# Layer 0's norm products on GpSimd, negated sines on ScalarE, six table stores for eight

## The chip, the cores and the metric

The kernel runs on one core of a Trainium2 chip. The metric is the device time of one execution in microseconds; the time shown is the median of several runs. The core's engines are TensorE (PE, matrix products), VectorE (DVE), ScalarE (ACT), GpSimd (POOL) and SyncE (SP), which issues nearly all transfers here. Each engine works through its own queue in order.

## The reference

A two-layer encoder on 2048 tokens of width 1024. Each layer takes `hn = rms_norm(x, norm_gain)`, projects it to 4096 columns, runs a banded attention over eight heads of 64 and a chunked retention with rotary phases over four heads of 128, gates both, and adds the product with `w_out` to `x`. A last norm ends it. The two pieces that the change touches are these:

```python
def rms_norm(x, gain=None):
    xf = x.astype(jnp.float32)
    y = xf * lax.rsqrt(jnp.mean(xf * xf, axis=-1, keepdims=True) + EPS)
    if gain is not None:
        y = y * gain.astype(jnp.float32)

def rotary_tables(positions, dim):
    inv_freq = 1.0 / (ROPE_BASE ** jnp.linspace(0.0, 1.0, dim // 2, dtype=jnp.float32))
    ang = positions.astype(jnp.float32)[:, None] * inv_freq[None, :]
    return jnp.cos(ang), jnp.sin(ang)
```

## The kernel before

The 2048 tokens are 16 tiles of 128 (tokens 0 to 15 in the names: `rsn_9` belongs to tile 9). Four tiles make a column block of 512, so a layer has four blocks, n = 0 to 3. Weights come in sections; for each section and block PE computes `dT` (L731, columns of the projection as rows, for queries and keys) and then `dV` (L752, values and gates). The attention and retention of the block before run in between, in thirds. Every f32 operand of a matrix product is split into a high and a low half in f16, `hi` on ScalarE and `lo` = value minus hi on VectorE.

The normed tokens of layer 0 are made once, in section 0, ahead of the block that uses them. For one tile of 128 x 1024: ScalarE squares and sums a row (`sq`), VectorE scales the sum (L210) and GpSimd raises it to the power -1/2 (L212), which gives the root factor `rsn`; then VectorE multiplies x by the row's factor and by the gain `gb` (`mul`, L254 or L1207), in place; ScalarE writes hi (L227 or L269), VectorE lo (L231 or L276), and SP transposes both by DMA into the block's tiles `hTh` and `hTl` (L236, L237). Tiles 0 to 3 take a way of their own through PE, which the change leaves. Tiles 4 to 7 are steps `x...4` to `x...7` in a string of step names that is the order of the program's start (L1388 on), and tiles 8 to 15 come from `norms_from_input` (L1192), where a list gives each tile's steps one round each, interleaved with attention and retention.

Rotary needs a cosine and a signed sine table per block, 128 x 512 each. `tables` (L84) computes angles of 256 positions on each of two halves of 64 partitions, reduces them in steps on VectorE (L93 to L119), takes sine and cosine on ScalarE (L121, L122), negates the sine on VectorE (L124), and stores to device memory by eight stores of 64 x 256 (L129 to L132): the cosine twice, the negated and the plain sine once each, for both halves. `dense_T` loads them back as `tabc` and `tabs` (L616, L617); the rotary products with them are L670, with `swp`, the swapped halves. There are four such sets, for n = 0 to 3.

PE, ACT, DVE and POOL execute in the order of the code. SP's order is the code's as far as the end of the first block's `dV`, and after that a planner places the transfers by its own costs.

What else the prediction names: `S` scores (L800), their maximum `mq` (L804, L806), the exponents (L807) and halves `pq` on ScalarE (L809) and GpSimd (L810), transposes `pT` of them by SP (L812); gates `v`, `rv`, `gt` (ACT L760 to L763, DVE L766 to L770), which free the accumulator that the next `dV` needs; `sh`, the retention state's halves (L864, L868), and `rss` its root (L920, L921).

Of the kernel before, what the change touches and what calls it, by code (L numbers as in the profile page):

```python
# [12 lines left out]
AF = mybir.ActivationFunctionType  # L13
ALU = mybir.AluOpType
# [13 lines left out]
def hybrid_trunk(ctx: ExitStack, tc: tile.TileContext, x, pos, gain, gcol, w_in, w_out, rel, fgain,  # L28
# [8 lines left out]
    act, dve, pool, pe, sp = nc.scalar, nc.vector, nc.gpsimd, nc.tensor, nc.sync  # L37
# [32 lines left out]
    tab_d = [dp.tile([2, P, 512], F32, tag=f"tab{n}", name=f"tab{n}") for n in range(NS)]  # L70
# [12 lines left out]
    def tables(n, wk):  # L83

        ang, k, r, k2 = wk
        pi = k2.bitcast(I32)
        for hf in range(2):
            o = n * 512 + hf * 256
            sp.dma_start(pi[hf * 64:(hf + 1) * 64, :], pos[None, o:o + 256].to_broadcast([64, 256]))
        yield  # L90

        def mulsub(dst, kk, c):
            dve.scalar_tensor_tensor(out=dst, in0=kk, scalar=-c, in1=dst, op0=ALU.mult, op1=ALU.add)  # L93

        def rnd(dst, src, mul):
            dve.tensor_scalar(dst, src, mul, MAGIC, op0=ALU.mult, op1=ALU.add)
            dve.tensor_scalar(dst, dst, -MAGIC, None, op0=ALU.add)

        dve.tensor_copy(ang, pi)
        dve.tensor_scalar(ang, ang, invf_sb[:, 0:1], None, op0=ALU.mult)  # L100
        yield
        rnd(k, ang, 1.0 / P1)
        yield
        for c in (PA, PB, PC):
            mulsub(ang, k, c)
            yield
        dve.tensor_scalar(k2, k, -(PD + PE_), None, op0=ALU.mult)
        dve.tensor_tensor(k2, k2, ang, op=ALU.add)
        yield
        rnd(k2, k2, 1.0 / TWO_PI)  # L110
        yield
        for kk, c in ((k2, QA), (k, PD), (k2, QB), (k, PE_), (k2, QC)):
            mulsub(ang, kk, c)
            yield
        dve.tensor_scalar(ang, ang, PI_CL, -PI_CL, op0=ALU.min, op1=ALU.max)
        dve.tensor_scalar(k, ang, HALF_PI, -TWO_PI, op0=ALU.is_gt, op1=ALU.mult)
        yield
        dve.tensor_tensor(k, k, ang, op=ALU.add)
        dve.tensor_scalar(k, k, HALF_PI, PI_CL, op0=ALU.add, op1=ALU.min)  # L119
        yield  # L120
        act.activation(r, ang, AF.Sin)  # L121
        act.activation(k2, k, AF.Sin)  # L122
        yield
        dve.tensor_scalar(ang, r, -1.0, None, op0=ALU.mult)  # L124
        yield
        for hf in range(2):
            sl = slice(hf * 64, hf * 64 + 64)
            cs = slice(hf * 256, hf * 256 + 256)
            sp.dma_start(tab_d[n][0, 0:64, cs], k2[sl, :])  # L129
            sp.dma_start(tab_d[n][0, 64:128, cs], k2[sl, :])  # L130
            sp.dma_start(tab_d[n][1, 0:64, cs], ang[sl, :])
            sp.dma_start(tab_d[n][1, 64:128, cs], r[sl, :])  # L132
        tab_done.add(n)
        yield

# [18 lines left out]
    gains = {}  # L154
# [48 lines left out]
    def squares(xt, nm, junk):  # L203
        ss = b2.tile([P, 1], F32, tag="ss", name=f"ss{nm}", bufs=4)
        act.activation(junk, xt, AF.Square, accum_out=ss)
        return ss

    def rms_of(ss, m, e, nm):

        dve.tensor_scalar(ss, ss, m, e, op0=ALU.mult, op1=ALU.add)  # L210
        rs = b2.tile([P, 1], F32, tag="rs", name=f"rs{nm}", bufs=4)
        pool.tensor_tensor(rs, ss, mhalf, op=ALU.pow)  # L212
        return rs

    def hT_of(l, n):
        if (l, n) not in hT:
            hT[l, n] = (hp.tile([P, KT, 512], F16, tag="hTh", name=f"hTh{l}_{n}"),
                        hp.tile([P, KT, 512], F16, tag="hTl", name=f"hTl{l}_{n}"))
        return hT[l, n]

    def row_pair(nm):
        return (b2.tile([P, 1280], F16, tag="sc", name=f"rh{nm}")[:, 0:D],
                b2.tile([P, 1280], F16, tag="pq", name=f"rl{nm}")[:, 0:D])

    def rows_hi(rows, xt, s_=None):

        act.activation(rows[0], xt, AF.Copy, scale=1.0 if s_ is None else s_[:, 0:1])  # L227

    def rows_lo(rows, xt, s_=None):
        if s_ is None:  # L230
            dve.tensor_tensor(rows[1], xt, rows[0], op=ALU.subtract)  # L231
        else:
            dve.scalar_tensor_tensor(out=rows[1], in0=xt, scalar=s_[:, 0:1], in1=rows[0], op0=ALU.mult, op1=ALU.subtract)

    def transpose_rows(rows, dh, dl):
        sp.dma_start_transpose(out=dh, in_=rows[0])  # L236
        sp.dma_start_transpose(out=dl, in_=rows[1])  # L237

    class Tok:
# [11 lines left out]
            self.r = rms_of(self.ss, gains[0].m, gains[0].e, self.nm)  # L251

        def mul(self):
            dve.scalar_tensor_tensor(out=self.x, in0=self.x, scalar=self.r[:, 0:1], in1=gains[0].b, op0=ALU.mult,  # L254
                                     op1=ALU.mult)

# [9 lines left out]
        def hi(self):  # L266
            if self.rows:
                self.rw = (self.rows[:, 0:D], self.rows[:, D:2 * D])
                act.activation(self.rw[0], self.x, AF.Copy)  # L269
                return  # L270
            for h in range(2):
                act.activation(self.hh[:, h * KT // 2:(h + 1) * KT // 2, :], self.pt[h], AF.Copy)

        def lo(self):
            if self.rows:
                dve.tensor_tensor(self.rw[1], self.x, self.rw[0], op=ALU.subtract)  # L276
                return
            for h in range(2):
                ks = slice(h * KT // 2, (h + 1) * KT // 2)
                dve.tensor_tensor(self.hl[:, ks, :], self.pt[h], self.hh[:, ks, :], op=ALU.subtract)  # L280
# [871 lines left out]
    def push(gen, steps):  # L1152
        bg.append([gen, steps])
# [36 lines left out]
    def norms_from_input(ts, spaces, tab):  # L1190

        def load(k):  # L1192
            u = us[k]
            u.x = spaces[k] if spaces else w4.tile([P, D], F32, tag="w4", name=f"xin{u.t}")
            sp.dma_start(u.x, x[u.t * P:(u.t + 1) * P, :])

        def sq(k):
            u = us[k]
            u.h = [h_[:, :, u.t % 4 * P:(u.t % 4 + 1) * P] for h_ in hT_of(0, u.t // 4)]
            u.ss = squares(u.x.rearrange("p (k c) -> p k c", c=P), u.nm, u.h[0])  # L1200

        def root(k):
            us[k].rs = rms_of(us[k].ss, gains[0].m, gains[0].e, us[k].nm)

        def mul(k):
            u = us[k]
            dve.scalar_tensor_tensor(out=u.x, in0=u.x, scalar=u.rs[:, 0:1], in1=gains[0].b, op0=ALU.mult, op1=ALU.mult)  # L1207

        def hi(k):
            us[k].rows = row_pair(us[k].nm)  # L1210
            rows_hi(us[k].rows, us[k].x)

        def lo(k):
            rows_lo(us[k].rows, us[k].x)

        def dma(k):
            transpose_rows(us[k].rows, *us[k].h)

        us = []
        for t in ts:  # L1220
            u = St()
            u.t, u.nm = t, f"n0_{t}"
            us.append(u)
        plan = {0: [lambda: load(0)]}
        add = lambda r, fn, k: plan.setdefault(r, []).append(lambda: fn(k))
        for k in range(4):
            if k:
                add(4 * k - 4, load, k)
            for i, fn in enumerate((sq, root, mul, hi, lo, dma)):
                add(3 + 4 * k + i, fn, k)  # L1230
        for r in range(21):
            for fn in plan.get(r, ()):
                fn()
            next(tab, None)
            yield
        for _ in tab:
            yield
# [58 lines left out]
    gain_load(0)  # L1296
    sp.dma_start(invf_sb, invf)
    t0 = tables(0, [gp.tile([P, 256], F32, tag="gt", name=f"wk{i}") for i in range(4)])
    go_on(t0)
    W.load(0)  # L1300
# [77 lines left out]
    def do(names):  # L1378
        for nm in names.split():
            steps[nm]()  # L1380

    def rounds(lists):
        for names in lists:
            do(names)
            yield
# [1 line left out]
    do("xsq0 xrs0 t xmul0 t t t t xtr0 Wsq0 xhi0 Wlp0 Wsc0 xsq1 xlo0 Whi0 xrs1 xsq2 Wlo0 t xsq3 xmul1 d Wsq1 xrs2 xrs3 xtr1 "  # L1387
# [3 lines left out]
    g00.vdone = 4  # L1391
    push(rounds(["xhi4 xrs5 xrs6", "xlo4 xmul5 xrs7", "xdma4 xhi5 xmul6 bt", "xlo5 xhi6 u", "xdma5 xlo6 xmul7", "xdma6 xhi7",
                 "xlo7", "xdma7 u", "u u bt", "u u bt", "u u", "u u bt"]), 12)
    att = [None]
    for l in range(DEPTH):
        gO = [Grp(), Grp()]
        go = Grp()
        for s in range(NSW):
            g = grp(l, s)
            for n in range(NS):  # L1400
# [6 lines left out]
                if n == 0 and not first:  # L1407
                    bs, bt = bias_scratch(l, s), bias_tiles(l, s, g)
# [21 lines left out]
                if n == NS - 1 and s == NSW - 1:  # L1430
                    us = []
# [108 lines left out]
```

## Time and profile before

| what | value |
|---|---|
| runs | 2083.72, 2083.68, 2080.86 us, median 2083.68 |
| profiled execution | 2085.9 us, its span 2084.1 |
| PE busy | 2005.3 us, 96% |
| VectorE busy | 1345.9 us, 65% |
| ScalarE busy | 1141.0 us, 55% |
| GpSimd busy | 435.8 us, 21% |
| stretch that the change touches | from 0 to about 215 us |

Times are microseconds from the start of the span. In a row of the timeline, the first number is the start, the second the length, then engine, line, operation, destination and sources, and shape; in brackets stands how long the engine was idle before and what ended that. SPq rows are issues of transfers, whose length is the issue and not the transfer. In a row of waits the numbers are the total, the count and the longest.

### The profile page before, as it was taken

The page shows a single profiled execution, that of the slowest core. Times are in us where ns is not written, and L with a number is a line of the kernel's source. Part 1 is how long each engine was busy: PE and PEld are TensorE (multiplying, and loading weights), DVE is VectorE, ACT ScalarE, POOL GpSimd, SP SyncE. Part 2 cuts the span into 40 slices and gives each one's busy share as a digit, 9 for nine tenths or more (in the row PEclk, how much of TensorE's full clock was granted, in tenths as well). Part 3 has the DMA queues.
Part 4 walks back from the last instruction along what each step waited for, and adds up shares of the span by engine and source line. Part 5 has one row for each costly group of instructions (what it writes and reads, how often), then busy time and mean ns, then how long its engine had stood idle before and what let it go on. Part 6 is the DMA issues. An engine that isn't in the chain of part 4 may idle for free. (4 is left out here: it accounts for less than half of the span.)

```text
span 2084.1 us, 39559 instructions
## 1 busy us (share of the span) xinstructions
PE 2005.3 (96%) x14014; PEld 1051.2 (50%) x14014; DVE 1345.9 (65%) x4031; ACT 1141.0 (55%) x2522; POOL 435.8 (21%) x509
## 2 busy tenths in 40 slices
PE   6888999999999999999999999999999999999998
PEld 4334454555555555544444555555555555555443
DVE  7677666666666666676654667666666666667643
ACT  7455565556565654565444546554655665446432
POOL 1022221222122222231000222222222222222100
PEclk9999999999999999999999999999999999999999
DMA  8767775557567764699875556655755766557874
GB/s 250 169 121 164 142 158 113 120 102 158 121 147 147 158 158 99 134 221 256 219 187 118 121 102 138 134 120 102 149 125 125 174 153 166 121 117 176 212 199 124
DMA packets 645702, 313.65 MB, mean 150 GB/s; under 512 B 459232, under 2 KB 602080, under 8 KB 645504
## 3 DMA queue, kind: packets, MB, share of 16 engines
q1 hardware_dynamic: 645504, 311.12, 66.3%
q8 instruction: 110, 1.80, 0.4%
q14 instruction: 88, 0.72, 0.1%
HBM read 123.26 MB, written 41.98 MB: 79 GB/s over the span
## 5 line engine op out<-in xcount | busy, mean ns | idle before, releaser
L810 POOL TENSOR_TENSOR pq<-sc,pq 128x640 f16<-128x640 f32 (+4 forms) x256 | 324.7, 1269 | 1165.6 <-issue 625.4
L807 ACT ACTIVATE sc<-sc,mq,cT 128x640 f32<-128x640 f32 (+4 forms) x256 | 218.5, 853 | 552.0 <-DVE mq L806 416.9
L731 PE MATMUL dT<-hTh,whT 128*128 128x512 f16 x1008 | 351.5, 385 | 15.8 <-DMA hTh<-hTl 9.7
L752 PE MATMUL dV<-whV,hTh 128*128 128x512 f16 x1024 | 352.9, 380 | 10.0 <-DVE gt L770 9.9
L752 PE MATMUL dV<-whV,hTl 128*128 128x512 f16 x1024 | 353.0, 380 | 0.0
L752 PE MATMUL dV<-wlV,hTh 128*128 128x512 f16 x1024 | 352.7, 380 | 0.0
L731 PE MATMUL dT<-hTh,wlT 128*128 128x512 f16 x1008 | 346.6, 379 | 0.0
L731 PE MATMUL dT<-hTl,whT 128*128 128x512 f16 x1008 | 346.6, 379 | 0.0
L752 PEld LDWEIGHTS <-hTh 128*128 128x128 f16 x2048 | 196.6, 98 | 223.1 <-DVE gt L770 13.7
L731 PEld LDWEIGHTS <-whT 128*128 128x128 f16 x2016 | 193.2, 98 | 223.8 <-issue 26.9
L804 DVE CUSTOM_DVE_ANT_0 sc<-S,bias 128x640 f32<-128x640 f32 (+4 forms) x256 | 188.6, 737 | 70.5 <-PE S L801 64.5
L809 ACT ACTIVATE pq<-sc 128x640 f16<-128x640 f32 (+4 forms) x256 | 171.5, 670 | 10.5 <-DMA pT<-pq 2.5
L1129 PE MATMUL dO<-whO,yly 128*128 128x512 f16 x448 | 170.3, 380 | 2.2 <-DMA yly<-rly 1.5
L1129 PE MATMUL dO<-whO,yhy 128*128 128x512 f16 x448 | 170.3, 380 | 0.4 <-DMA yhy<-hTh 0.4
L1129 PE MATMUL dO<-wlO,yhy 128*128 128x512 f16 x448 | 170.2, 380 | 0.0
L752 PEld LDWEIGHTS <-hTl 128*128 128x128 f16 x1024 | 99.5, 98 | 104.0 <-issue 1.4
L731 PEld LDWEIGHTS <-wlT 128*128 128x128 f16 x1008 | 97.3, 98 | 101.8 <-issue 1.1
L800 PE MATMUL S<-k,q 128*128 128x128 f16 (+3 forms) x592 | 143.3, 268 | 1.9 <-DVE mq L804 1.8
L1129 PEld LDWEIGHTS <-yhy 128*128 128x128 f16 x896 | 87.5, 98 | 101.9 <-issue 1.1
L820 PE MATMUL o<-v,pT 128*128 128x65 f16 x1120 | 130.4, 194 | 8.1 <-DMA pT<-pq 7.6
L821 PE MATMUL o<-v,pT 128*128 128x64 f16 x1120 | 130.6, 195 | 0.0
L801 PE MATMUL S<-k,q 128*128 128x128 f16 (+3 forms) x592 | 130.4, 268 | 0.0
(361 smaller groups left out, 3412.0 us busy)
## 6 DMA issues: line engine op xcount, KB each, us to landing
q<-qq SPq DMA_DIRECT2D x128, 128.0 KB, 2.6
yyy<-y_d SPq DMA_DIRECT2D x32, 512.0 KB, 4.7
stT<-in_w_in_dram SPq DMA_DIRECT2D x27, 512.0 KB, 4.6
stV<-in_w_in_dram SPq DMA_DIRECT2D x26, 512.0 KB, 4.6
k<-kk SPq DMA_DIRECT2D x128, 64.0 KB, 2.0
swp<-rot SPq DMA_DIRECT2D x64, 128.0 KB, 2.5
tabc<-tab SPq DMA_DIRECT2D x32, 256.0 KB, 2.7
tabs<-tab SPq DMA_DIRECT2D x32, 256.0 KB, 2.9
```

Source lines behind the costliest of these rows:

```text
L731: pe.matmul(ps, w_[:, j, kt, :], h_[:, kt, :], start=(m == 0), stop=(m == 23))
L752: pe.matmul(ps, h_[:, kt, a * P:(a + 1) * P], w_[:, kt, :], start=(m == 0), stop=(m == 23))
L800: pe.matmul(o, st.q[:, hx, 0, cs], k_, start=True, stop=False)
L801: pe.matmul(o, st.q[:, hx, 1, cs], k_, start=False, stop=True)
L804: dve.tensor_tensor_reduce(out=v, in0=S[:, 0:w], in1=g.bias[hx][:, 640 - w:640], scale=1.0, scalar=-3.0e38, op0=ALU.add, op1=ALU.max, accu ...
L807: act.activation(v, v, AF.Exp, bias=m[:, 0:1], scale=g.c[:, 0:1])
L809: act.activation(pq[:, 0:w], v, AF.Copy)
L810: pool.tensor_tensor(pq[:, w:2 * w], v, pq[:, 0:w], op=ALU.subtract)
L820: pe.matmul(o[:, 0:65], u.p[:, b, :], v_[:, 0:65], start=(b == 0), stop=False)
L821: pe.matmul(o[:, 0:64], u.p[:, b, :], v_[:, 65:129], start=False, stop=False)
L1129: pe.matmul(ps, h_[:, kt, :], w_[:, kt, :], start=(m == 0), stop=(m == 23))
```

## The change

For tiles 4 to 15 the product with the gain moves from VectorE to GpSimd, and it no longer contains the row's factor: GpSimd computes x times gain in place, right behind the square (ahead of the root instead of behind it). The row's factor enters as a scale of the split: hi is ScalarE's copy with scale r, and lo is VectorE's (x times r) minus hi in one instruction. For each of the four table sets the sine's negation is a ScalarE copy with scale -1 behind the two sines, in place of a VectorE instruction two steps later. The cosine's two stores become one of 64 x 2 x 256 with the source doubled, so a set has six stores instead of eight.

```diff
         act.activation(r, ang, AF.Sin)
         act.activation(k2, k, AF.Sin)
-        yield
-        dve.tensor_scalar(ang, r, -1.0, None, op0=ALU.mult)
-        yield
+        act.activation(ang, r, AF.Copy, scale=-1.0)
+        yield
+        yield
+        d = tab_d[n].rearrange("i (b p) (a c) -> i b a p c", b=2, a=2)
         for hf in range(2):
             sl = slice(hf * 64, hf * 64 + 64)
-            cs = slice(hf * 256, hf * 256 + 256)
-            sp.dma_start(tab_d[n][0, 0:64, cs], k2[sl, :])
-            sp.dma_start(tab_d[n][0, 64:128, cs], k2[sl, :])
-            sp.dma_start(tab_d[n][1, 0:64, cs], ang[sl, :])
-            sp.dma_start(tab_d[n][1, 64:128, cs], r[sl, :])
+            sp.dma_start(d[0, :, hf].rearrange("b p c -> p b c"), k2[sl, None, :].to_broadcast([64, 2, 256]))
+            for b, t_ in enumerate((ang, r)):
+                sp.dma_start(d[1, b, hf], t_[sl, :])
...
         def mul(self):
+            if self.rows:
+                pool.tensor_tensor(self.x, self.x, gains[0].b, op=ALU.mult)
+                return
...
-                act.activation(self.rw[0], self.x, AF.Copy)
+                rows_hi(self.rw, self.x, self.r)
...
-                dve.tensor_tensor(self.rw[1], self.x, self.rw[0], op=ALU.subtract)
+                rows_lo(self.rw, self.x, self.r)
...
         def mul(k):
-            u = us[k]
-            dve.scalar_tensor_tensor(out=u.x, in0=u.x, scalar=u.rs[:, 0:1], in1=gains[0].b, op0=ALU.mult, op1=ALU.mult)
+            pool.tensor_tensor(us[k].x, us[k].x, gains[0].b, op=ALU.mult)
...
-            rows_hi(us[k].rows, us[k].x)
+            rows_hi(us[k].rows, us[k].x, us[k].rs)
...
-            rows_lo(us[k].rows, us[k].x)
+            rows_lo(us[k].rows, us[k].x, us[k].rs)
...
-            for i, fn in enumerate((sq, root, mul, hi, lo, dma)):
+            for i, fn in enumerate((sq, mul, root, hi, lo, dma)):
```

The string of steps for tiles 4 to 7 is changed in the same sense: `xmul4` to `xmul7` stand behind the squares.

The order of PE is the same in both kernels. Three places show what moves elsewhere. First SP's queue ahead of the last transposes of block 1, before:

```order
L1195 DMA hTh_3_152<-in_x_dram 128x1024
L1195 DMA hTl_3_153<-in_x_dram 128x1024
L666 DMA swp_0_0_3_904<-raw_0_0_779 64x512
L667 DMA swp_0_0_3_904<-raw_0_0_779 64x512
L236 DMA_TRANSPOSE hTh_1_148<-hTl_2_151 128x8x128
L237 DMA_TRANSPOSE hTl_1_149<-hTl_2_151 128x8x128
L577 DMA bias_1_947<-toep_1_523 128x640
L1195 DMA hTl_3_153<-in_x_dram 128x1024
```

and now:

```order
L1197 DMA hTh_3_152<-in_x_dram 128x1024
L668 DMA swp_0_0_3_902<-raw_0_0_779 64x512
L669 DMA swp_0_0_3_902<-raw_0_0_779 64x512
L235 DMA_TRANSPOSE hTh_1_148<-hTl_2_151 128x8x128
L236 DMA_TRANSPOSE hTl_1_149<-hTl_2_151 128x8x128
L579 DMA bias_1_945<-toep_1_523 128x640
L1197 DMA hTl_3_153<-in_x_dram 128x1024 x2
```

The two transposes are those of tile 7, and the load of tile 10's input (into `hTl_3`) has moved from ahead of them to behind them. Next GpSimd's queue beside the attention of block 0, where tiles 10 and 11 are normed, before:

```order
L810 TENSOR_TENSOR pq_0_0_2_0_1336<-sc_0_0_2_0_1331,pq_0_0_2_0_1336 128x384
L212 TENSOR_TENSOR rsn_10_1365<-ssn_10_1341,mhalf 128x1
L921 TENSOR_TENSOR rss_0_1_1298<-rss_0_1_1298,mhalf 128x1
L810 TENSOR_TENSOR pq_0_0_2_1_1421<-sc_0_0_2_1_1416,pq_0_0_2_1_1421 128x384
L212 TENSOR_TENSOR rsn_11_1489<-ssn_11_1451,mhalf 128x1
L810 TENSOR_TENSOR pq_0_0_3_0_1523<-sc_0_0_3_0_1518,pq_0_0_3_0_1523 128x512
```

and now:

```order
L812 TENSOR_TENSOR pq_0_0_2_0_1332<-sc_0_0_2_0_1327,pq_0_0_2_0_1332 128x384
L1208 TENSOR_TENSOR hTl_3_153<-hTl_3_153,gb_160 128x1024
L923 TENSOR_TENSOR rss_0_1_1294<-rss_0_1_1294,mhalf 128x1
L211 TENSOR_TENSOR rsn_10_1384<-ssn_10_1337,mhalf 128x1
L812 TENSOR_TENSOR pq_0_0_2_1_1417<-sc_0_0_2_1_1412,pq_0_0_2_1_1417 128x384
L1208 TENSOR_TENSOR hTl_3_153<-hTl_3_153,gb_160 128x1024
L812 TENSOR_TENSOR pq_0_0_3_0_1517<-sc_0_0_3_0_1512,pq_0_0_3_0_1517 128x512
L211 TENSOR_TENSOR rsn_11_1522<-ssn_11_1447,mhalf 128x1
```

Each product (L1208) stands in front of its root, and tile 11's root now comes behind the attention's `pq_0_0_3_0`. Last VectorE's queue at tile 14, where PE waits for `sh` and then for the gates, before:

```order
L832 TENSOR_SCALAR ya_0_1_1_0_2117<-o_0_1_1_0_2064,rl_0_1_1_0_2114,gt_0_1_1_1464 128x64
L1207 TENSOR_SCALAR xin_1816<-xin_1816,rsn_14_2099,gb_160 128x1024
L115 TENSOR_SCALAR xb<-xb 128x256
L116 TENSOR_SCALAR xb<-xb 128x256
L676 TENSOR_TENSOR rot_0_2_2_1931<-rot_0_2_2_1931 128x512
L868 TENSOR_SCALAR sh_0_5_2040<-sh_0_5_2040,state_0_0_1129 128x128
```

and now:

```order
L834 TENSOR_SCALAR ya_0_1_1_0_2109<-o_0_1_1_0_2058,rl_0_1_1_0_2106,gt_0_1_1_1461 128x64
L209 TENSOR_SCALAR ssn_14_2037<-ssn_14_2037,gm_231,ge_232 128x1
L115 TENSOR_SCALAR xb<-xb 128x256
L116 TENSOR_SCALAR xb<-xb 128x256
L678 TENSOR_TENSOR rot_0_2_2_1925<-rot_0_2_2_1925 128x512
L870 TENSOR_SCALAR sh_0_5_2034<-sh_0_5_2034,state_0_0_1125 128x128
```

The product is gone from here, and the scaling of the row's sum (`ssn_14`), which stood five instructions earlier, has come into its place.

More of the change, by code (lines that the diff above doesn't have):

```diff
@@ L1389, in hybrid_trunk @@
        "t Vlp0 Whi2 Vsc0 t xlo3 Whi3 bs t d Vhi0 Wlo2 d Vhi1 Wlo3 t d d d Vlo0 t Vsq2 d Vlo1 t Vsq3 d Vlp2 d Tu Vsc2 xsq4 "
[1 row of a table removed]
[1 row of a table added]
     g00.vdone = 4
-    push(rounds(["xhi4 xrs5 xrs6", "xlo4 xmul5 xrs7", "xdma4 xhi5 xmul6 bt", "xlo5 xhi6 u", "xdma5 xlo6 xmul7", "xdma6 xhi7",
+    push(rounds(["xhi4 xrs5", "xlo4 xrs6 xmul7", "xdma4 xhi5 xrs7 bt", "xlo5 xhi6 u", "xdma5 xlo6", "xdma6 xhi7",
                  "xlo7", "xdma7 u", "u u bt", "u u bt", "u u", "u u bt"]), 12)
```

2 rows, old and new, of the table steps are left out of this document.

## The prediction

> **What bounds the kernel now.** I read the page first, for the engine that fills the span, and then the waits of that engine in the stretch that the change touches.
>
> ```profile
> span 2084.1 us, 39559 instructions
> PE 2005.3 (96%) x14014; PEld 1051.2 (50%) x14014; DVE 1345.9 (65%) x4031; ACT 1141.0 (55%) x2522; POOL 435.8 (21%) x509
> ```
>
> PE is busy for 96% of the span, so an edit on another engine moves the time only where PE waits for it. Every edit belongs to tokens 4 to 15 of layer 0 or to the sine tables, and both are used up by about 215 us. The waits of PE by line, and by what it waited for (us in total, times, longest), in three windows: 50 to 110, 110 to 160 and 160 to 216 us.
>
> ```profile
> PE dT L731 <- DMA hTh<-hTl: 9.7, 1, 9.7
> ...
> PE dV L752 <- DVE gt L770: 5.5, 2, 4.9
> PE dT L731 <- issue: 2.4, 1, 2.4
> ...
> PE dT L731 <- DMA hTh<-rhn: 3.6, 1, 3.6
> PE dV L752 <- DVE gt L770: 3.2, 2, 2.7
> PE r L860 <- DVE sh L868: 1.9, 1, 1.9
> ```
>
> At most 26 us are in play (9.7 + 5.5 + 2.4 + 3.6 + 3.2 + 1.9), in three places, where PE goes from column block 0 to 1 (A), from 1 to 2 (B) and from 2 to 3 (C). In each it waits for the last transposed token of the next block or for VectorE's gates. A long wait has a tail: behind it the granted clock stands at half. In the next view the columns are the busy times of PE, its weight load, VectorE, ScalarE and GpSimd, then the granted clock and the DMA engines' share.
>
> ```profile
> 58.00:78.00 20.00, 10.80 (x50) 4.50 (x47) 10.91 (x22) 7.08 (x17) 0.29 (x2) 0.85 1.04 228
> 80.00:82.00 2.00, 2.00 (x7) 0.72 (x6) 1.97 (x7) 0.83 (x1) 0.29 (x2) 0.50 0.63 249
> 106.00:126.00 20.00, 16.03 (x94) 7.48 (x91) 17.39 (x45) 11.27 (x24) 3.39 (x6) 1.00 0.52 95
> ```
>
> Before A the DMA engines are full (share 1.04) and VectorE is half idle; before B VectorE is 87% busy. The two halves of the change therefore meet different limits: fewer stores can help A, and work taken off VectorE can help B and C.
>
> **The prices.** Groups by line and shape; the number behind the comma is the mean of one in ns.
>
> ```profile
> L1207 DVE SCALAR_TENSOR_TENSOR hTh<-hTh,rsn,gb 128x1024 f32<-128x1024 f32 x2 | 2.6, 1281 | 2.0 <-POOL rsn L212 2.0
> L231 DVE TENSOR_TENSOR rln<-hTh,rhn 128x1024 f16<-128x1024 f32 x2 | 2.4, 1216 | 0.0
> L1349 DVE SCALAR_TENSOR_TENSOR wlV<-hTl,sc2V,whV 128x1024 f16<-128x1024 f32 x2 | 2.5, 1280 | 0.9 <-ACT whV L1346 0.9
> ...
> L227 ACT ACTIVATE rhn<-xin 128x1024 f16<-128x1024 f32 x4 | 4.2, 1044 | 1.3 <-DVE xin L1207 1.3
> L227 ACT ACTIVATE rhy<-yyy,sy 128x1024 f16<-128x1024 f32 x10 | 11.4, 1144 | 21.9 <-DVE iy L149 17.1 <-DVE oscy L977 4.8
> ...
> L1058 POOL TENSOR_TENSOR hTl<-hTl,fg 128x512 f32<-128x512 f32 x1 | 1.3, 1262 | 3.9 <-ACT fj L1054 3.9
> L810 POOL TENSOR_TENSOR pq<-sc,pq 128x640 f16<-128x640 f32 x192 | 271.7, 1415 | 861.0 <-issue 469.1 <-ACT pq L809 374.0 <-DMA y_d<-ya 11.2
> ```
>
> Per token VectorE loses a 1.28 us product (some 1.2 us of its queue, since neighbours overlap slightly) and its subtraction grows from 1.22 to 1.28. ScalarE's first half grows from 1.04 to 1.14, because it takes a per-row scale. GpSimd gains a product of 128x1024 that the trace does not show. Twice L1058 gives 2.5 us as an upper end; L810 scaled by its elements gives 1415 x 1024/640 = 2.26. I take 2.25, since L810 has 192 instances. Twelve of them are 27 us on an engine that is 79% idle, so GpSimd itself is no bound.
>
> VectorE may still not be free while GpSimd multiplies. Three instructions of the timeline (start, length):
>
> ```profile
> 107.74 0.16 DVE L827 TENSOR_TENSOR rl<-rl,kaV 128x1 f32<-128x1 f32 x1
> ...
> 188.00 1.38 DVE L827 TENSOR_TENSOR rl<-rl,kaV 128x1 f32<-128x1 f32 x1
> ...
> 187.97 1.40 POOL L810 TENSOR_TENSOR pq<-sc,pq 128x640 f16<-128x640 f32 x1 [4.54 <-ACT pq L809]
> ```
>
> The same one-column product takes 0.16 us alone, and 1.38 us where it starts 0.03 us behind a GpSimd product; it ends with that one (189.38 against 189.37). I read this as the two engines excluding each other for products with two SBUF operands. A GpSimd product can thus hold VectorE for up to 2.25 us, in return for 1.2 us freed, wherever VectorE's queue brings a two-operand instruction in that time. The Trainium skill, "GPSIMD Engine Reference", § 8 Key points, says the same in general: GpSimd shares its SBUF interfaces with VectorE, with contention against VectorE instructions that have two SBUF inputs, and VectorE is about twice as fast at elementwise work. By that page alone the product would cost some 2.6 us (an estimate, twice 1.28) and the move would be a loss wherever VectorE is the limit; the row above agrees on the holding. The rival that follows from it is the second one below.
>
> **A, from block 0 to 1.** SP's issues and PE's restart:
>
> ```profile
> 48.30 0.60 SPq L129 DMA_DIRECT2D tab<-wk  x1
> ...
> 52.77 0.59 SPq L132 DMA_DIRECT2D tab<-wk  x1
> ...
> 70.95 0.41 SPq L1195 DMA_DIRECT2D hTl<-in_x_dram  x1
> ...
> 72.70 1.54 SPq L236 DMA_TRANSPOSE hTh<-hTl  x1
> ...
> 78.52 3.57 PE L731 MATMUL dT<-hTh,whT 128*128 128x512 f16 x8 [9.69 <-DMA hTh<-hTl]
> ```
>
> Eight stores of a table take one issue every 0.64 us ((52.77 - 48.30)/7). SP issues without a gap from there to the transpose of token 7 at 72.70, which PE waits for; the token's rows were split several us earlier. Two issues fewer are -1.28 us, if a store with a doubled source costs the same 0.6. If it costs two, nothing is saved; I take 0.6, because the bytes of a destination row stay as they were. The load of token 10's input leaves its place ahead of token 7's transposes, which is -0.41 us and half a megabyte out of the full DMA stretch. Sum -1.7 at SP. Landing is limited by the DMA engines too, so between 0 and -3.5 (both, with the load's own transfer out of the way); I take -1.6. The half-clock stretch behind the wait lasts 3.6 us, and its end may stay where it is: up to 1.7 us either way, for the range alone. GpSimd's four products of tokens 4 to 7 lie before 66 us under VectorE's slack, and cost nothing; without that cover, four times 1.05 us.
>
> **B, from 1 to 2.** VectorE's queue resumes at 106.93, and then runs nearly full:
>
> ```profile
> 106.93 0.69 DVE L670 TENSOR_TENSOR rot<-rot,tabc 128x512 f32<-128x512 f32 x1 [3.22 <-DMA swp<-rot]
> ...
> 115.19 0.41 DVE L93 SCALAR_TENSOR_TENSOR xb<-xb 128x256 f32<-128x256 f32 x1
> ...
> 129.06 0.41 DVE L770 SCALAR_TENSOR_TENSOR gt<-gt,dV 128x256 f32<-128x256 f32 x1
> ...
> 129.57 0.29 DVE L124 TENSOR_SCALAR xb<-xb 128x256 f32<-128x256 f32 x1
> ...
> 113.84 0.91 POOL L810 TENSOR_TENSOR pq<-sc,pq 128x384 f16<-128x384 f32 x1 [7.50 <-ACT pq L809]
> ...
> 132.62 1.15 POOL L810 TENSOR_TENSOR pq<-sc,pq 128x512 f16<-128x512 f32 x1 [2.33 <-issue]
> ...
> 125.97 0.40 ACT L122 ACTIVATE xb<-xb 128x256 f32<-128x256 f32 x1
> ...
> 136.18 1.87 SPq L236 DMA_TRANSPOSE hTh<-rhn  x1
> ```
>
> SP's two issues fewer could let VectorE resume 1.28 earlier, but token 9's product on GpSimd starts at about 105.8 and holds L670 or what follows it until about 108; with its own 1.2 us removed, VectorE is then where it was. Token 10's product follows the GpSimd instruction of 113.84, so it runs from 114.8 to 117.0, and the instruction of 115.19 has two operands and waits: +1.8 us, against -1.2 for the removed product behind it. That is +0.6 on the way to ScalarE's next exponent. Then the negated sine stands on ScalarE ahead of the gates: its neighbour of the same size, L122, holds the queue some 0.32 us, so the gates of 129.06, and PE with them, are +0.9 later. VectorE's 0.29 at L124 comes behind the gates and frees nothing that PE waits for. Token 11's root now stands behind the GpSimd product of 132.62; its first half ends by about 136.0, beside the issue at 136.18. There SP has two stores fewer: between -1.28 and +1. I take -0.2 for B where PE takes token 11 up.
>
> **C, from 2 to 3.**
>
> ```profile
> 180.00 1.28 DVE L1207 SCALAR_TENSOR_TENSOR xin<-xin,rsn,gb 128x1024 f32<-128x1024 f32 x1 [2.55 <-POOL rsn L212]
> ...
> 194.18 1.28 DVE L1207 SCALAR_TENSOR_TENSOR xin<-xin,rsn,gb 128x1024 f32<-128x1024 f32 x1
> ...
> 178.06 1.40 POOL L810 TENSOR_TENSOR pq<-sc,pq 128x640 f16<-128x640 f32 x1 [8.00 <-ACT pq L809]
> ...
> 196.69 0.92 ACT L807 ACTIVATE sc<-sc,mq,cT 128x640 f32<-128x640 f32 x1 [2.31 <-DVE mq L806]
> ...
> 201.32 3.12 SPq L236 DMA_TRANSPOSE hTh<-rhn  x1
> ```
>
> VectorE waits 2.55 us for token 14's root, then multiplies; both go, 3.8 us. But the product now runs on GpSimd from 179.46 to 181.7, and the next VectorE instructions (the rotary split, the state L868 that PE waits 1.9 us for) have two operands: the wait only changes its name, 0 (between +0.5 and -1.9). Then the gates of the second wait: ScalarE's chain +0.32. Token 15's product at 194.18 leaves VectorE, which brings the exponent of 196.69 1.2 earlier, less the 0.32: -0.9. It leads through the attention weights to SP's issue of token 15 at 201.32, where two stores fewer are already saved. C -0.8.
>
> **The sum.** -1.6 - 0.2 - 0.8 = -2.6 us. The profiled execution took 2085.9 us (span 2084.1 and 1.8 around it), 2.2 above the median of 2083.68. So 2083.3 beside it, and 2081.1 in the runs.
>
> **The rivals.**
> - *VectorE really gains.* If its queue mostly finds instructions with one operand while GpSimd works, it keeps the 1.2 us of tokens 9 and 10 and the 3.8 of token 14. Then A -3.5, B -1.3 (SP's lead), C -3.0 (the 1.9 us wait gone, and 1.1 of the 2.7): -7.8, 2075.9. For it: GpSimd is idle 79%. Against it: L93, L676 and L868 stand right where the products fall.
> - *GpSimd holds VectorE (slower).* Each of tokens 9, 10, 14 and 15 costs 2.25 - 1.2 = 1.05, and each of two chains the 0.32, while A gets nothing since the transposes are limited by the DMA engines: +4.8, 2088.5; one more half-clock stretch makes it 2090. It decides once the products of tokens 10 and 14 both delay the gates by more than 1.2 us. For it: the row of 188.00.
> - *The stores do not get cheaper.* A doubled store issues like two: A and C lose 1.3 each, total 0, 2083.7.
>
> **How the numbers follow.** About 0.2% (4.2 us) is what a measurement of this kernel tells from no change. Forecast 0.44 (2078.5 to 2084.0; 0.10 of it under 2079.5), VectorE gains 0.24 (all faster), held 0.25 (0.22 of it above 2087.9), stores no cheaper 0.07 (same). Faster 0.34, same 0.44, slower 0.22. Range 2074.5, a little under the gaining case, to 2089.0, a little over the held one; about 0.2 lies outside.
>
> **What would show it.** PE's row of 78.52 should come at about 77, with SP's table stores six to a set, 0.6 us each, and a GpSimd product of 128x1024 near 2.25 us. VectorE's L93 and L676 should appear stretched to the end of such a product. PE's wait for the gates near 129.5 should grow to about 5.5, and the waits near 206 shrink by about 0.8. I am wrong if the doubled store takes 1.2 us, if the product takes over 3 us, or if no VectorE instruction is stretched.

## The result, and the profile after

The changed kernel takes 2080.08 us (median), the kernel before 2083.69. The ratio is 0.9982, with a 95% interval from 0.9975 to 0.9989; a second measurement on another chip gave 0.9977 (0.9968 to 0.9987). So it is faster by some 0.2%, 3.6 and 4.0 us by the medians. The forecast of 2081.1 was 1 us above.

The profiled execution took 2076.7 us, 3.4 under its own median, and the profile before lies 2.2 over its median. The two traces therefore differ by 9.2 us, of which over half is the chance of two executions. Below, a second profile of each kernel stands beside the first, and the totals go by medians alone.

The page of the changed kernel:

```profile
span 2074.9 us, 39558 instructions
PE 2001.0 (96%) x14014; PEld 1048.7 (51%) x14014; DVE 1347.7 (65%) x4015; ACT 1143.1 (55%) x2526; POOL 462.8 (22%) x521
```

GpSimd gained 27 us, and VectorE, which lost twelve products, is busy 1.8 us *longer*. The timeline shows why. VectorE and GpSimd, in the changed kernel, at tiles 9, 10 and 14:

```profile
101.78 2.85 DVE L672 TENSOR_TENSOR rot<-rot,tabc 128x512 f32<-128x512 f32 x1 [1.62 <-ACT raw L664]
...
110.99 2.51 DVE L93 SCALAR_TENSOR_TENSOR xb<-xb 128x256 f32<-128x256 f32 x1
...
175.58 2.43 DVE L870 SCALAR_TENSOR_TENSOR sh<-sh,state 128x128 f16<-128x128 f16 x1
...
101.73 2.34 POOL L1208 TENSOR_TENSOR hTh<-hTh,gb 128x1024 f32<-128x1024 f32 x1
...
110.86 2.35 POOL L1208 TENSOR_TENSOR hTl<-hTl,gb 128x1024 f32<-128x1024 f32 x1
...
175.07 2.79 POOL L1208 TENSOR_TENSOR xin<-xin,gb 128x1024 f32<-128x1024 f32 x1
```

Three VectorE instructions of 0.69, 0.41 and 0.28 us are stretched until GpSimd's product is over (110.86 + 2.35 = 113.21, and L93 ends at 113.50). The freed time is counted as busy in other instructions. All three have two operands in SBUF. At tile 4 an instruction with one operand and a scalar per row, which takes 0.28 us elsewhere, is stretched too:

```profile
40.78 2.33 DVE L351 TENSOR_SCALAR msk<-msk,rdc 128x128 f32<-128x128 f32 x1
...
40.69 2.35 POOL L254 TENSOR_TENSOR hTh<-hTh,gb 128x1024 f32<-128x1024 f32 x1 [19.84 <-ACT hTh L247]
```

Instructions that read the accumulators in PSUM, and those with one operand of one column, ran beside the products at their usual length (at 56.75, for instance, the gates' L772 took 0.41 us inside a product that ran from 56.21 to 58.57).

PE's waits after, in the windows of the prediction:

```profile
PE dT L733 <- DMA hTh<-hTl: 6.4, 1, 6.4
...
PE dV L754 <- DVE gt L772: 4.3, 2, 3.8
PE r L862 <- DVE sh L870: 1.8, 1, 1.8
...
PE dV L754 <- DVE gt L772: 3.5, 2, 2.9
PE dT L733 <- DMA hTh<-rhn: 2.7, 1, 2.7
PE r L862 <- DVE sh L870: 1.9, 1, 1.9
```

At A the wait fell from 9.7 to 6.4 us. At B the gates' wait fell from 5.5 to 4.3, and a wait of 1.8 for the retention state came up, behind the stretched L93. At C the wait for the last transposes fell from 3.6 to 2.7, and the gates' wait rose from 3.2 to 3.5. SP and PE at A:

```profile
48.12 0.66 SPq L129 DMA_DIRECT2D tab<-wk  x1
...
69.78 1.53 SPq L235 DMA_TRANSPOSE hTh<-hTl  x1
...
74.94 0.58 PE L733 MATMUL dT<-hTh,whT 128*128 128x512 f16 x1 [6.41 <-DMA hTh<-hTl]
```

The first doubled store takes 0.66 us and the second of the set 0.60, where a single store takes 0.60. From the first table store to PE's restart it is now 26.8 us (74.94 - 48.12), against 30.2 before (78.52 - 48.30).

### The profile page after: what moved, and what is told of

Same layout as the page of the kernel before. It is cut to its first block, busy times and chain, and to the rows that moved or that the text cites. A ratio compares the mean times of both kernels' runs of the same rounds, so it can differ in the third digit from the quotient of the medians.

```text
span 2074.9 us, 39558 instructions
## 1 busy us (share of the span) xinstructions
PE 2001.0 (96%) x14014; PEld 1048.7 (51%) x14014; DVE 1347.7 (65%) x4015; ACT 1143.1 (55%) x2526; POOL 462.8 (22%) x521
## 3 DMA queue, kind: packets, MB, share of 16 engines
q1 hardware_dynamic: 645376, 311.12, 67.1%
## 5 line engine op out<-in xcount | busy, mean ns | idle before, releaser
L802 PE MATMUL S<-k,q 128*128 128x128 f16 (+3 forms) x592 | 142.6, 267 | 1.0 <-DVE mq L806 0.9
L822 PEld LDWEIGHTS <-pT 128*128 128x128 f16 x1120 | 105.6, 97 | 48.4 <-DMA pT<-pq 20.2
```

Source lines behind the costliest of these rows:

```text
L802: pe.matmul(o, st.q[:, hx, 0, cs], k_, start=True, stop=False)
L822: pe.matmul(o[:, 0:65], u.p[:, b, :], v_[:, 0:65], start=(b == 0), stop=False)
```

## The experiments

The first four do or undo one part at a time. The place A is measured from the first table store to PE's restart. The place B is measured from the first to the ninth GpSimd instruction of the attention weights, which spans the change from block 1 to 2.

**Six stores alone.**

```diff
-            sp.dma_start(tab_d[n][0, 0:64, cs], k2[sl, :])
-            sp.dma_start(tab_d[n][0, 64:128, cs], k2[sl, :])
+            sp.dma_start(d[0, :, hf].rearrange("b p c -> p b c"), k2[sl, None, :].to_broadcast([64, 2, 256]))
```

> Only the six stores for eight; products and negation stay on VectorE. Theory S (the gain is SP's two issues fewer): PE takes up block 1 about 1.3 us earlier than 78.5, blocks 2 and 3 some 1.0 earlier each, the median about 2.5 us under the kernel before. Theory P (the gain is the products leaving VectorE and the input load that moves with them): within 1 us of before.

Measured: 2079.74 us, 0.9982 (0.9973 to 0.9991): as much as the whole change, and 3.6 us under before, which is more than either theory expected. But the gain is not where the change has it. PE restarts at 77.3, theory S's 1.3 us ahead of the first profile's 78.5; counted from the first table store, whose own time differs from run to run, A is 28.9 us, against 30.2 and 29.0 in the two profiles of before. B is 59.5 (142.04 - 82.57), against 63.7 and 61.8 before and 62.3 in the whole change.

```profile
82.57 0.53 POOL L809 TENSOR_TENSOR pq<-sc,pq 128x128 f16<-128x128 f32 x1 [2.99 <-ACT pq L808]
...
142.04 1.40 POOL L809 TENSOR_TENSOR pq<-sc,pq 128x640 f16<-128x640 f32 x1 [4.17 <-ACT pq L808]
```

The same two rows of the kernel before:

```profile
84.01 0.52 POOL L810 TENSOR_TENSOR pq<-sc,pq 128x128 f16<-128x128 f32 x1 [3.05 <-ACT pq L809]
...
147.66 1.40 POOL L810 TENSOR_TENSOR pq<-sc,pq 128x640 f16<-128x640 f32 x1 [6.40 <-ACT pq L809]
```

And of the whole change:

```profile
80.37 0.53 POOL L812 TENSOR_TENSOR pq<-sc,pq 128x128 f16<-128x128 f32 x1 [2.81 <-ACT pq L811]
...
142.71 1.40 POOL L812 TENSOR_TENSOR pq<-sc,pq 128x640 f16<-128x640 f32 x1 [3.60 <-ACT pq L811]
```

**The products alone.** Eight stores and VectorE's negation, the rest as in the change.

```diff
-            dve.scalar_tensor_tensor(out=u.x, in0=u.x, scalar=u.rs[:, 0:1], in1=gains[0].b, op0=ALU.mult, op1=ALU.mult)
+            pool.tensor_tensor(us[k].x, us[k].x, gains[0].b, op=ALU.mult)
```

> Only the products on GpSimd, with the roots as scales; eight stores, negation on VectorE. The input load of tile 10 stands behind tile 7's transposes as in the whole change. Theory S: between 1 us faster and 1 us slower, since GpSimd's 2.35 us products hold VectorE as long as they free it. Theory P: 2.5 to 3.5 us faster, PE's restart at block 1 at about 76.

Measured: 2077.73 us, 0.9973 (0.9964 to 0.9982). PE restarts at 75.5, where theory P had about 76, but the 5.6 us by the medians are more than both theories allowed (at most 1 and 3.5). A took 27.2 us, B 62.2. So the products help at A, where GpSimd's work was expected to do nothing, and do not help at B. A accounts for 1.8 to 3.0 of the 5.6; where the rest lies is open.

**The negation alone.**

```diff
-        dve.tensor_scalar(ang, r, -1.0, None, op0=ALU.mult)
+        act.activation(ang, r, AF.Copy, scale=-1.0)
```

> Only the negated sine on ScalarE. Both theories: the gates near 129 and 193 come 0.3 us later, the median 0 to 0.7 us above before.

Measured: 2082.39 us, 0.9997 (0.9988 to 1.0006), no change; A 29.2, B 61.8, both as before.

**The change without its negation.**

```diff
-        act.activation(ang, r, AF.Copy, scale=-1.0)
+        dve.tensor_scalar(ang, r, -1.0, None, op0=ALU.mult)
```

> The whole change without its negation on ScalarE (back on VectorE). Both theories: 0 to 0.7 us under the whole change, so 3.6 to 4.3 under before. If the sum of the single parts falls short of this, the parts help each other (an SP lead is used only where the tokens come earlier too).

Measured: 2074.90 us, 0.9964 (0.9951 to 0.9978), some 8 us under before where 3.6 to 4.3 were expected. The single gains of stores and products (0.18 and 0.27%) nearly add to the 0.36% here. That left the negation to cost some 4 us in company while it costs nothing alone. A possible reason was the clock: in this kernel PE works until 72.6 at A, and the granted clock stays at 1.00, while in the whole change it stands at 0.50 from 74 to 76 us.

**The whole change again**, to have both beside each other.

> The whole change once more, beside the kernel before on this chip, to set against the change without its negation (0.9964 of before). If the negation on ScalarE costs in company what it does not cost alone, this stays at about 0.998, 3 us or more above; if the two differ by chance only, it comes down to 0.9965 to 0.9975.

Measured: 2078.27 us, 0.9977 (0.9968 to 0.9987). A 26.9 and B 62.2, as in the first profile and as without the negation (26.8 and 62.2). The ratio lies between the two expectations, 0.0013 above that without the negation, and the two intervals overlap. Neither A nor B shows a place for a difference.

**PE kept warm at A.**

```diff
+            if j == 0 and (l, s, n) == (0, 0, 1):
+                for i in range(20):
+                    pe.matmul(ps, g.h[:, 0, i % KT, :], hT[0, n - 1][0][:, i % KT, :], start=True, stop=True)
```

> The whole change with 20 products more on PE ahead of block 1 (into the accumulator that the first real product starts anew), which fill some 4 us of the 6.4 us wait. Theory C (the difference between the whole change and the change without negation is the half-clock stretch behind that wait, which the other kernel escapes since its PE is busy till 72.6): the first eight products of block 1 take 1.9 us instead of 3.2, and the median falls 1.3 to 2 us under the whole change. Rival: the restart comes later by as much, no change or slower by up to 1 us.

Measured: 2083.28 us, 1.0005 (0.9996 to 1.0014), slower than the whole change. The clock did what theory C says, and it was worth nothing. PE's rows at the restart, and the first attention weights:

```profile
68.68 4.48 PE L729 MATMUL dT<-hTh,whT 128*128 128x512 f16 x20
...
76.32 1.02 PE L736 MATMUL dT<-hTh,whT 128*128 128x512 f16 x4 [3.16 <-DMA hTh<-hTl]
...
81.80 0.52 POOL L815 TENSOR_TENSOR pq<-sc,pq 128x128 f16<-128x128 f32 x1 [2.27 <-ACT pq L814]
```

Four products take 1.02 us, at a granted clock of 1.00, but the first attention weights come 5.5 us behind the restart here, and also 5.5 behind it in the second profile of the whole change, where the clock was at 0.50: PE waits 1.4 us for the rotation instead. Theory C falls. The median's rise comes from elsewhere: in the traces the lead over before shrinks from 6.3 us to nothing between about 533 and 1128 us, in a stretch in which the order of the queues is the same as in the whole change: 4.0 of it between 690 and 740 us, 2.0 between 900 and 1129. Why is open.

**The products of tiles 4 to 7 alone, and of tiles 8 to 15 alone**, both with six stores and VectorE's negation. The first restores these lines of the tiles 8 to 15, the second those of the tiles 4 to 7:

```diff
         def mul(k):
-            pool.tensor_tensor(us[k].x, us[k].x, gains[0].b, op=ALU.mult)
+            u = us[k]
+            dve.scalar_tensor_tensor(out=u.x, in0=u.x, scalar=u.rs[:, 0:1], in1=gains[0].b, op0=ALU.mult, op1=ALU.mult)
...
         def mul(self):
-            if self.rows:
-                pool.tensor_tensor(self.x, self.x, gains[0].b, op=ALU.mult)
-                return
```

> Six stores, and the products of tiles 4 to 7 alone on GpSimd; tiles 8 to 15 and the negation stay on VectorE. The input load of tile 10 stands behind tile 7's transposes. Theory L (the products' gain is at block 1: load order and a PE that stays at full clock): within 1.5 us of the change without negation, about 7 to 8.5 us under before. Theory V (the gain is VectorE's relief at blocks 2 and 3): no better than the six stores alone, 3 to 4 us under before.

> Six stores, and the products of tiles 8 to 15 alone on GpSimd; tiles 4 to 7 and the negation stay on VectorE, and the load of tile 10 stays ahead of tile 7's transposes. Theory L: as the six stores alone, 3 to 4 us under before, since GpSimd holds VectorE for what it frees. Theory V: 6 us or more under before.

Measured: 2072.12 us, 0.9951 (0.9937 to 0.9964) for tiles 4 to 7; 2079.46 us, 0.9983 (0.9973 to 0.9992) for tiles 8 to 15. So theory V falls: tiles 4 to 7 alone give much more than the 3 to 4 us it allowed, and tiles 8 to 15 alone 2.8 us where it asked for 6. Theory L fits the second nearly; the first is 10.1 us under before, more than L's 7 to 8.5, because B is shorter too. With tiles 4 to 7 alone A takes 25.7 us and B 58.5 (138.69 - 80.17); with tiles 8 to 15 alone A takes 29.4, B 62.2 (146.08 - 83.90):

```profile
80.17 0.52 POOL L812 TENSOR_TENSOR pq<-sc,pq 128x128 f16<-128x128 f32 x1 [2.90 <-ACT pq L811]
...
138.69 1.41 POOL L812 TENSOR_TENSOR pq<-sc,pq 128x640 f16<-128x640 f32 x1 [3.24 <-ACT pq L811]
```

Of the 14 profiles here, the six with single GpSimd products for tiles 8 to 15 have B between 62.2 and 62.3, with six stores or with eight. The three with six stores, VectorE's products there and SP's order as the planner leaves it have 58.5 to 59.5. So the six stores shorten B, and the products of tiles 8 to 15 undo that.

**The same kernel again** (tiles 4 to 7 alone), on another chip.

> Six stores and the products of tiles 4 to 7 alone on GpSimd, once more beside the others: 7 to 10 us under before, and below the whole change.

Measured: 2073.44 us, 0.9951 (0.9939 to 0.9963). A 26.3, B 59.0. It lies under before as clearly as the first time, and again its interval ends below both of the whole change.

**The kernel before again**, for its profile.

> The kernel before once more, for a second profile of it. If the half-clock stretches behind its waits near 140 and 207 us are the chance of one execution, they are missing or shorter here, and PE reaches the time after block 3 some 2 to 3 us earlier than in the first profile; the way from the first table store to PE's restart at block 1 should stay near 30 us.

Its span is 2080.4 us, 3.7 under the first. A took 29.0 us (30.2 in the first profile), B 61.8 (63.7). The 17th GpSimd instruction of the attention weights starts at 213.5 instead of 215.0, so 1.5 us of the first profile's lead-up was chance, a little less than expected. The granted clock stands at 1.00 from 138 to 144 us, so the half-clock stretch there was chance; from 207 to 211 us it is 0.50 again.

**GpSimd's products twice** for tiles 8 to 15.

```diff
+            pool.tensor_tensor(us[k].h[0], us[k].x.rearrange("p (k c) -> p k c", c=P),
+                               gains[0].b.rearrange("p (k c) -> p k c", c=P), op=ALU.mult)
             pool.tensor_tensor(us[k].x, us[k].x, gains[0].b, op=ALU.mult)
```

> The whole change, and for tiles 8 to 15 each GpSimd product made twice (the first into a buffer that is overwritten later). If GpSimd's products hold VectorE, the gates near 115 and 180 come up to 2.4 us later each and the median rises 2 to 5 us over the whole change; if GpSimd's idle time covers them, it stays within 1 us.

Measured: 2084.75 us, 1.0008 (1.0000 to 1.0017), some 5.5 us over the whole change when both are set against before, a little over the 2 to 5 expected. B took 69.5 us (149.85 - 80.39), 7.1 more. VectorE and GpSimd at tile 10:

```profile
116.05 2.50 DVE L93 SCALAR_TENSOR_TENSOR xb<-xb 128x256 f32<-128x256 f32 x1
118.48 2.83 DVE L678 TENSOR_TENSOR rot<-rot 128x512 f16<-128x512 f32 x1
...
115.93 2.35 POOL L1208 TENSOR_TENSOR hTh<-hTl,gb 128x1024 f16<-128x1024 f32 x1
118.35 2.41 POOL L1210 TENSOR_TENSOR hTl<-hTl,gb 128x1024 f32<-128x1024 f32 x1
```

Each product holds one VectorE instruction, one after the other. The doubled product also delays the tile itself, through its root and its halves, but that is not what PE waits for. Its waits from 106 to 155 us are nearly all for VectorE, and none is for a tile's transposes:

```profile
PE dV L754 <- DVE gt L772: 5.8, 2, 5.3
PE S L802 <- DVE mq L806: 2.5, 1, 2.5
PE o L822 <- DVE ya L834: 2.0, 1, 2.0
PE r L862 <- DVE sh L870: 1.9, 1, 1.9
PE o L822 <- DMA pT<-pq: 0.5, 1, 0.5
```

An engine that is 77% idle adds its work to the time here, because it holds VectorE while it works.

**The load's place alone.** Six stores, everything else on VectorE, and tile 10's input load kept in program order.

```diff
+            i = sp.dma_start(u.x, x[u.t * P:(u.t + 1) * P, :])
+            if u.t == 10:
+                tc.keep_in_program_order(i)
```

> Six stores, all products and the negation on VectorE as before, and only the input load of tile 10 placed behind tile 7's transposes. If the products help at block 1 by this load's place alone, the time from tile 7's transpose to PE's restart is 5 us instead of 5.9, and the median is 5 to 8 us under before, against 3.5 for the stores alone; if it needs the products on GpSimd, it stays at 3 to 4 under before.

Measured: 2077.42 us, 0.9973 (0.9963 to 0.9984), 5.6 under before. The interval overlaps that of the stores alone (0.9973 to 0.9991), so the totals do not show what the load's place adds; A does. SP and PE:

```profile
69.70 1.60 SPq L235 DMA_TRANSPOSE hTh<-hTl  x1
...
74.80 3.57 PE L730 MATMUL dT<-hTh,whT 128*128 128x512 f16 x8 [6.01 <-DMA hTh<-hTl]
```

From tile 7's transpose to the restart it is 5.1 us. Over all profiles, that lag is 5.6 to 6.0 us wherever the load stands ahead of the transposes (five profiles) and 4.8 to 5.2 wherever it stands behind (nine). A is 27.3 here without any product on GpSimd, against 28.9 and 29.4 with six stores and the load ahead, and 26.8 and 26.9 in the whole change. So the products help at A for the most part by the place that SP's planner then gives to a load. The load stands deeper in SP's queue here than in the change (behind the next block's tables), some transposes of tile 8 moved with it, and B took 61.1 instead of 59.5.

## Why the prediction was right

The total was right in sign and nearly in size (-2.6 forecast, -3.6 and -4.0 measured); it lies near the 0.2% bound, where the forecast put it. That the sum came so near is partly luck: A gained more than its term, and of C's term at most some 0.3 us shows. By its own steps:

- **Prices.** GpSimd's product takes 2.34 to 2.81 us, 2.25 was taken; the doubled store takes 0.60 to 0.66, 0.6 was taken.
- **A, -1.6.** Right in sign, too small: A is 26.8 and 26.9 in the change, against 30.2 and 29.0 before, so -2.2 to -3.4. The terms were mis-sized, both ways. The stores, at -1.28, gave little here: A is 28.9 and 29.4 with them, 29.2 with eight stores and the negation alone. SP's lead is 1.2 us just behind the stores (the next issue comes 3.99 us behind the first store, against 5.17), but where SP issues tile 7's transposes it has mostly gone: with the load ahead, they come 22.9 and 23.5 us behind the first store with six, 24.4, 23.4 and 23.5 with eight. Two issues fewer thus did not bring the transposes 1.28 us forward, since other issues ahead of them took longer: one issue of tile 4's transposes and one of tile 5's take 2.10 and 3.19 us in the kernel with six stores alone, 1.36 and 3.02 in the second profile of before. The load's place, at -0.41 plus an unpriced share, gave 1.6 to 2.1: it takes SP's issue away and shortens the transposes' landing by 0.8 us.
- **B, -0.2.** Right. B is 62.2 to 62.3, and 61.8 and 63.7 before. The mechanism held too: VectorE's relief is cancelled, and L672 and L93 are the instructions held. But the cancelled sum was larger than thought. Six stores without GpSimd's products shorten B by 2.3 us or more, and the products of tiles 8 to 15 take that back, whether six stores or eight stand beside them (62.2).
- **The gates' wait near 129.5**, which was to grow to 5.5, shrank to 3.8 and 3.7. The gates did come 0.8 us later, counted from the first attention weights (126.25 - 80.37 against 129.06 - 84.01), where 0.9 was forecast. In that count the three kernels with GpSimd's products for tiles 8 to 15 and VectorE's negation have 45.5 us, the whole change 45.9 and 45.7, before 45.1 and 45.0. So the products cost 0.5 there (0.6 forecast) and the negation 0.2 to 0.4 (0.32 forecast). Against the three kernels with six stores and without these products, which have 43.3 to 43.7, they cost about 2: they take the stores' lead as well. But PE, after its new wait of 1.8 us for the state, came later still. The wait changed its name rather than its sum.
- **C, -0.8.** Not settled. From the ninth to the 17th GpSimd instruction of the weights, the whole change takes 64.5 and 66.1 us, before 67.3 and 67.1; but one and the same kernel (tiles 4 to 7 alone) takes 65.1 and 68.4, and the negation alone 64.5. Measured to PE's restart at block 3 it is 58.7 and 58.6, against 59.0 and 58.7 before. The wait there shrank as forecast, from 3.6 and 3.5 us to 2.7 and 2.2, but it is 2.6 with the six stores alone as well.
- **The negation, +0.32 at the gates.** Alone it costs nothing that is measurable. Without it the change reads 0.9964, with it 0.9982 and 0.9977, and the intervals overlap. The gates near 129.5 show 0.2 to 0.4 us, of which nothing is left at the end of B (62.2 to 62.3 with it and 62.2 without); whether some 3 us in the total are real stays open, as no place in the traces shows them.
- **The rivals.** "VectorE really gains" falls with B at 62.2 to 62.3 in every kernel with single GpSimd products for tiles 8 to 15. Its condition was too narrow as well: an instruction with one operand can be held like the others (L351, 2.33 us instead of 0.28). "GpSimd holds VectorE" is the right mechanism; it did not decide, because A gained. "The stores do not get cheaper" falls with 0.60 and 0.66 us.

The Trainium skill's sentence on shared SBUF interfaces ("GPSIMD Engine Reference", § 8 Key points) is borne out by the rows of 101.78, 110.99 and 175.58; its factor of two stands beside 2.35 against 1.28 us, 1.8.

## What to carry to other kernels

Work moved from VectorE to an idle GpSimd frees VectorE only where its next instructions are not held. Here those with two SBUF operands were held, and so was a one-operand instruction of 128 x 128, while those that read PSUM ran on. Look at what stands in VectorE's queue at that very place, and move the work where VectorE has slack anyway: with tiles 4 to 7 alone B takes 58.5 and 59.0 us, with all twelve 62.2 (the totals, 0.9951 twice against 0.9964 with the same stores and negation, have intervals that overlap). Where the transfer queue limits a stage, read what a planner puts ahead of the last transfer that is waited for: at A the place of one half-megabyte load was worth 1.6 to 2.1 us, two issues fewer at most 1.3. And take a second profile of the unchanged kernel before you explain a difference: the two here differ by 3.7 us.

## What the runs showed that was not expected

- The time from the span's start to the first table store varies from 46.8 to 50.0 us over 14 executions; that alone is nearly as much as the change gives.
- Half clock behind a wait cost nothing at A: the first eight products took 1.9 us instead of 3.6, and the attention weights came no earlier.
- With twenty extra products at 68.7 us, 6 us were lost in a stretch after 533 us whose queues were ordered alike; the cause was not found.
